# A hand-ordered fp32 encoder block: the fourth gate half's steps moved and spread, its two column blocks swapped, attention heads closer together, and the first projection's gated products kept in SBUF

## The chip, the cores and the metric

The kernel runs on one core of a Trainium2 chip. The metric is device time in microseconds (us); three runs of the kernel before gave 894.41, 894.84 and 895.23, median 894.84. One more run was recorded with a profile: it took 893.12, of which the profile's span is 891.3. All times below that are read off the trace count from the start of that span.

## The reference

One layer of a hybrid bidirectional encoder, for 256 tokens of width 2048, all in float32. A recurrent branch and an attention branch are projected, gated and summed, and the sum goes through an output projection.

```
z = rms_norm(x, norm_pre_w) @ w_in            # 2048 x 13312, split into the parts below
u_lru, g_lru, q, k, v, g_attn, m_lru, m_attn = split(z)
h   = rg_lru(conv(u_lru), forward) + rg_lru(conv(u_lru), backward)
y_a = h * silu(g_lru)                                   # branch A
y_b = windowed_gqa(rope(q), rope(k), v, sink) * silu(g_attn)   # branch B: 16 heads of 128, |i-j| <= 128
merged = sigmoid(m_lru) * (y_a @ w_proj_a) + sigmoid(m_attn) * (y_b @ w_proj_b)
out = x + rms_norm(merged @ w_out, norm_post_w)
```

## The kernel before, in words

**Precision.** Every float32 matrix is split into a high part that TensorE takes exactly (`wh`, a rounded copy made by ScalarE, line 219) and a low part (`wl`, the rest, made by VectorE, line 221). A product is three matmuls: high by high, high by low, low by high (`mm3`, lines 225 to 227). Weights are read once from HBM, so the kernel is a long stream of weight loads, splits and matmuls.

**Steps.** The order is written by hand in three lists, START, MERGE and OUT. An entry such as `p2.1` is one step: 1 MB of weights (128 x 2048 float32), used in two halves. The letters of MERGE: `p0` to `p3` are the four 512-column chunks of the first projection (`w_proj_a`), four steps each; `b0` to `b3` the same for the second (`w_proj_b`); `Am...` the fourth gate half, that is the upper 1024 columns of `m_attn`; `Om...` the first steps of the output projection. A `p` or `b` step is a "quad": 24 matmuls, and it counts as two ticks. An `Am` step is a "part": 12 matmuls and one tick. Steps are numbered through all three lists: `p0.0` is step 114, `b0.0` step 134, `b1.0` step 142, and the weight load of step 142 is called `raw142`, its split halves `wh142_0`, `wl142_0`, `wh142_1`, `wl142_1`.

**The gate halves.** The four halves L, M, N and A of the gate projections, and half of the output projection, multiply 2 x 2 blocks with seven products instead of eight (class `Seven`, m1 to m7). Sums of weight blocks that this needs are made by the DMA engines: a cell `x` is loaded by SyncE's queue (SP) and then the next block is added onto it in place by an accumulating DMA on GpSimd's queue (POOL, line 192: `Ax0a`, `Ax0b`, `Ax1a`, `Ax1b`, and the same for `y`). Sums of activation blocks lie in DRAM and come back through SP (line 337, `Am50`, `Am30`, ...). The seven products end in two column blocks of 512: the left one is complete with m2 (first tokens) and m4 (last tokens), the right one with m3 and m6, and m7.

**Around the steps.** `at(tick, fn)` puts other work at a tick: it is written into each engine's stream ahead of that tick's matmuls. Each engine runs its stream in order. For each step the load is issued three steps ahead (line 207, a ring of three 1 MB buffers `raw`), the cast four halves ahead, the subtraction three halves ahead. All other large tiles come from one pool of 45 slots, `units` (each 128 x 1024 float32); whoever gets a slot waits for the last reader of the tile that had it. What doesn't fit is parked in DRAM and fetched back (`park`, line 790, and `back`, line 794, both on SP).

**The merge.** `add_pa` (lines 940 to 946) multiplies a chunk of the first projection by its gate in the tile `tm[c]` and parks the result (`parkpa`); at `b{c}.0` it is fetched back as `pa` (line 1018). `add_pb` multiplies a chunk of the second projection by the gate `sm[c]` and adds `tm[c]` (VectorE, lines 951 and 952); one tick later `turn` transposes the sum on TensorE (line 963, tile `mt`). The heads of group c start at `p0.0` - 16 + 12c ticks, three ticks apart: `scores`, `expo` (VectorE, line 871), `exps` (ScalarE, lines 877 and 878), `normalise` (ScalarE, line 885), then `flip` on TensorE (line 891, tile `pt`), five ticks after the scores.

Of the kernel before, what the change touches and what calls it, by code (L numbers as in the profile page):

```python
# [21 lines left out]
P = 128  # L22
D = 2048
S = 256
# [6 lines left out]
DECAY = 12  # L31
SPIN = 10
HEAD0 = -16
STRIDE = 3
FIRST = 8
QAWAY = 10
QPARK = (0,)
# [1 line left out]
U0, GL0, Q0, K0, V0, GA0, ML0, MA0 = 0, 2048, 4096, 6144, 6656, 7168, 9216, 11264  # L39
# [14 lines left out]

MERGE = """p0.0 p0.1 p0.2 p0.3 p1.0 p1.1 p1.2 p1.3 p2.0 p2.1 p2.2 p2.3 Am1.0 p3.0 p3.1 Am1.1 p3.2 Am2.0 p3.3 Am2.1 b0.0
    Am5.0 b0.1 Am5.1 b0.2 Am3.0 b0.3 Am3.1 b1.0 b1.1 Am6.0 b1.2 Am6.1 b1.3 Am7.0 b2.0 Am7.1 b2.1 Am4.0 b2.2 Am4.1
    b2.3 b3.0 Om1.0 b3.1 Om5.0 b3.2 b3.3""".split()
OUT = """o2.0 o2.1 Om1.1 o2.2 Om5.1 Om2.0 o2.3 Om3.0 Om6.0 Om3.1 o3.0 Om6.1 Om2.1 o3.1 Om7.0 Om7.1 Om4.0 Om4.1  # L60
    o3.2 o3.3""".split()

# [8 lines left out]
QUADS = {"u": ("w_in", U0), "v": ("w_in", V0), "p": ("w_proj_a", 0),  # L71
         "b": ("w_proj_b", 0), "o": ("w_out", 0)}
PAIRS = {"g": GL0, "h": GA0, "w": U0, "k": K0, "q": Q0}
SEVENS = {"L": ("w_in", ML0 + 1024), "M": ("w_in", ML0), "N": ("w_in", MA0), "A": ("w_in", MA0 + 1024), "O": ("w_out", 0)}


PV_NORM = 0
# [9 lines left out]
def load_plan():  # L87

    plan = []
    for o in START + MERGE + OUT:  # L90
        a, i = o.split(".")
        if a[0] in SEVENS:
            plan.append(("part", a[0], a[1:], int(i)))
# [9 lines left out]
def content(p):  # L103
    if p[0] == "part":
        _, g, a, q = p
        m, c = SEVENS[g]
        b, f = SEVEN[a][2]
        return "part", m, c + f * 512, b, q
    return p


# [4 lines left out]
def body(ctx, tc, x, xT, wall, wlru, pvec, npost, ident_d, mask_d, rope_d, out):  # L116
# [18 lines left out]
    def half_unit(name, tag, dt=F32, bufs=2):  # L135
        return small.tile([P, 2, S], dt, tag=tag, name=name, bufs=bufs)
# [25 lines left out]
    def at(hs, fn):  # L162
        assert hs >= now[0], (hs, now[0])
        due.setdefault(hs, []).append(fn)

    first, last = {}, {}
# [7 lines left out]
    def soon(fn, d=1):  # L174
        at(now[0] + d, fn)
# [276 lines left out]
    xs = []  # L452
# [167 lines left out]
    sgl, sga = [], []  # L620
    ya, yb = [None] * 8, [None] * 8
# [117 lines left out]
    tm, sm, ms, msum = {}, {}, {}, {}  # L739


    def gate_unit(gates, c):
        if c not in gates:
            gates[c] = unit(f"mg{c}", F32, (P, 2, 512))
        return gates[c]

    def gated_out(gates, c, t):
        if t == 1 and (gates is tm or c < 2):
            soon(lambda: park("tm" if gates is tm else "sm", gates, c), 5)
# [7 lines left out]
    def combine(to, ps, other, sign):  # L757
        nc.vector.scalar_tensor_tensor(to, ps, float(sign), other, ALU.mult, ALU.add if sign > 0 else ALU.subtract)

    def gate_sum(gates, first=2):  # L760

        def done(t, c, ps, other, sign):
            to = gate_unit(gates, first + c)[:, t]

            def gate(src):
                nc.scalar.activation(to, src, AF.Sigmoid, scale=rtok[:, t:t + 1])
                gated_out(gates, first + c, t)

            if other is None:
                gate(ps)  # L770
            else:
                combine(to, ps, other, sign)
                soon(lambda: gate(to))
        return done
# [1 line left out]
    Seven("L", xs, None, gate_sum(tm))  # L776
    Seven("M", xs, None, gate_sum(tm, 0))
    Seven("N", xs, None, gate_sum(sm, 0))
    Seven("A", xs, None, gate_sum(sm))
    for n in range(8):  # L780
        behind(XSUM[n], lambda n=n: x_sums(n))

# [2 lines left out]
    def park(key, store, c):  # L785

        d = parked[key, c] = dram.tile([P, 1024], F32, name=f"park{key}{c}")
        t = store[c]
        store[c] = None
        nc.sync.dma_start(d, flat(t))  # L790

    def back(key, store, c, shape=(P, 2, 512)):
        store[c] = unit(f"{key}{c}", F32, shape)
        nc.sync.dma_start(flat(store[c]), parked[key, c])
# [58 lines left out]
    def head(hd, qh, ql, b, both, end):  # L853

        g, j = hd // 4, hd % 4
        sk = pv[:, PV_SINK + hd:PV_SINK + hd + 1]
        ts = [slice(t * P, (t + 1) * P) for t in range(2)]
        v = {}

        def scores():  # L860
            v["sc"] = bank(f"sc{hd}")
            for t in range(2):
                mm3(v["sc"][:, t], qh[:, j, ts[t]], ql[:, j, ts[t]], kv["kh"][:, g], kv["kl"][:, g], True, True)

        def expo():
            p = v["p"] = half_unit(f"p{hd}", "p")
            sc = v.pop("sc")
            m, nm, es = tiny(f"m{hd}"), tiny(f"nm{hd}"), tiny(f"es{hd}")
            dn = v["dn"] = tiny(f"dn{hd}")
            for t in range(2):  # L870
                nc.vector.tensor_tensor_reduce(p[:, t], sc[:, t], table["mask"][:, t], rtok_sc[:, t:t + 1], sk, ALU.add, ALU.max, m[:, t:t + 1])  # L871
            nc.vector.tensor_scalar(nm, m, -1.0, None, ALU.mult)  # L872
            soon(lambda: exps(p, nm, es, dn))

        def exps(p, nm, es, dn):
            for t in range(2):
                nc.scalar.activation(p[:, t], p[:, t], AF.Exp, bias=nm[:, t:t + 1], accum_out=dn[:, t:t + 1])  # L877
            nc.scalar.activation(es, nm, AF.Exp, bias=sk)
            v["es"] = es

        def normalise():
            dn, rd = v["dn"], tiny(f"rd{hd}")
            nc.vector.tensor_tensor(dn, dn, v["es"], ALU.add)
            nc.vector.reciprocal(rd, dn)
            soon(lambda: [nc.scalar.activation(v["p"][:, t], v["p"][:, t], AF.Copy, scale=rd[:, t:t + 1]) for t in range(2)])

        def flip():
            v["pt"] = bank(f"pt{hd}")
            for kt in range(2):
                for t in range(2):  # L890
                    nc.tensor.transpose(v["pt"][:, kt, ts[t]], v["p"][:, t, ts[kt]], ident)  # L891

        def p_parts():
            if j % 2 == 0:
                both.update({s: unit(f"p{s}{hd}", F32R, (P, 2, 2, S)) for s in "hl"})
            parts_of(both["h"][:, :, j % 2], both["l"][:, :, j % 2], v.pop("pt"))
            v.clear()

        def values():
            both["o"] = bank(f"o{hd}")  # L900
            ks = slice(g * P, (g + 1) * P)
            for kt in range(2):
                mm3(both["o"], kv["vh"][:, kt, ks], kv["vl"][:, kt, ks], both["h"][:, kt], both["l"][:, kt], kt == 0, kt == 1)

        def gate_out():
            y = sga[g][:, j - 1:j + 1]
            nc.vector.tensor_tensor(y, both["o"], y, ALU.mult)
            both.clear()
            if j == 3 and g < 2:
                soon(lambda: park("yb", sga, g), 4)  # L910

        for d, fn in ((0, scores), (1, expo), (3, normalise), (5, flip), (6, p_parts)):
            at(b + d, fn)
        if j % 2 == 1:
            at(b + 10, values)
            at(b + 11, gate_out)
            if g > 1:
                at(max(b + 12, end + hd // 2 - 6), lambda: yb_parts(hd // 2))

    def yb_parts(q):  # L920
        yb[q] = pair_unit(f"yb{q}")
        n = q % 2 * 2
        parts_of(yb[q][:, :, 0], yb[q][:, :, 1], sga[q // 2][:, n:n + 2])

    def heads(g, b, end):
        def start():
            h, l = unit(f"qh{g}", F32R), unit(f"ql{g}", F32R)
            parts_of(h, l, qs.pop(g))
            soon(lambda: back("sga", sga, g, (P, 4, S)), 6)
            for j in range(4):  # L930
                if j % 2 == 0:
                    both = {}
                head(4 * g + j, h, l, b + STRIDE * j, both, end)

        if g in QPARK:
            at(b - 8, lambda: back("q", qs, g, (P, 4, S)))
        at(b - 2, start)


    def add_pa(c):  # L940
        def done(t, ps):
            nc.vector.tensor_tensor(tm[c][:, t], ps, tm[c][:, t], ALU.mult)
            if t == 1:
                soon(lambda: park("pa", tm, c), 4)

        add_rows(f"pa{c}_", ya, done)

# [67 lines left out]
    at(tick["q0.0"] - 6, load_tables)  # L1015
    for c in range(4):
        at(tick[f"p{c}.0"], lambda c=c: back("tm", tm, c))
        at(tick[f"b{c}.0"], lambda c=c: back("pa", tm, c))
        if c < 2:
            at(tick[f"b{c}.0"], lambda c=c: back("sm", sm, c))  # L1020
        heads(c, tick["p0.0"] + HEAD0 + 4 * STRIDE * c, tick["b0.0"])
    for c in range(4):
        if c < 3:
            at(tick["p0.0"] - 8 + 2 * c, lambda c=c: back("ya", sgl, c, (P, 4, S)))
        if c < 2:
            at(tick["b0.0"] - 12 + 3 * c, lambda c=c: back("yb", sga, c, (P, 4, S)))
    for n in range(8):
        if n < 6:
            at(tick["p0.0"] - 3 + n, lambda n=n: y_parts(n))
        if n < 4:  # L1030
            at(tick["b0.0"] - 6 + n, lambda n=n: yb_parts(n))


    npt, xr, yw = [], [[], []], [[], []]
# [16 lines left out]
    b, n = ticks(), ticks(len(plan))  # L1051
# [64 lines left out]
    tick = -1  # L1116
# [94 lines left out]
```

## Time and profile before

| what | value |
|---|---|
| median of three runs | 894.84 us |
| the profiled execution, its own time | 893.12 us |
| its span | 891.3 us |
| TensorE busy in the span | 875.4 us (98%) |
| TensorE weight loads | 750.4 us (84%) |
| VectorE | 711.4 us (80%) |
| ScalarE | 643.2 us (72%) |
| moved by DMA | 247.94 MB, mean 278 GB/s |
| granted TensorE clock, mean | 0.993 |

To read it: TensorE is called PE in the rows, VectorE DVE, ScalarE ACT, SyncE SP; an engine with a q behind its name is its queue or sequencer. A row of the timeline has the start, the length, the engine, the source line, the operation, what it writes and reads, and in brackets how long the engine had been idle before it and what ended that. A DMA row of SP or POOL shows the issue alone, not the transfer.

### The profile page before, as it was taken

To read this page: it belongs to the slowest core of one execution; us is meant where nothing else is said; L and a number is where in the kernel's file an instruction comes from. 1 tells how busy PE (TensorE), PEld (TensorE's weight loads), DVE (VectorE), ACT (ScalarE), POOL (GpSimd) and SP (SyncE) were. 2 spreads that over 40 slices of the span, in tenths; PEclk is the share of its full clock that TensorE was granted. 3 is DMA by queue.
4 is the path that set the end of the run, shared out by engine and by line. 5 is a ranking of instruction groups with operands and counts; after the bars stand their busy time and mean duration, and the time that the engine had idled before them with its cause. 6 is when DMAs were issued, how large, how long until landed. Compare 5 with 4: busy or idle time off the path is not lost.

```text
span 891.3 us, 12379 instructions
## 1 busy us (share of the span) xinstructions
PE 875.4 (98%) x4542; PEld 750.4 (84%) x4542; DVE 711.4 (80%) x959; ACT 643.2 (72%) x937; POOL 72.5 (8%) x104
## 2 busy tenths in 40 slices
PE   9999999999999999999999999999999799999996
PEld 8888888888888888888888888888888588888885
DVE  6899999898897987799688778766767377787776
ACT  7689697968787886977875899955575265555754
POOL 0000000011001011100011100000101110000200
PEclk9999999999999999999999999999999989999998
DMA  9657699999869999969899965776989999999962
GB/s 345 254 189 259 208 366 233 361 335 290 285 226 297 308 297 318 322 241 277 282 350 308 301 241 206 256 280 235 297 269 294 296 306 293 293 330 368 236 179 95
DMA packets 55838, 247.94 MB, mean 278 GB/s; under 512 B 5856, under 2 KB 10720, under 8 KB 40288
## 3 DMA queue, kind: packets, MB, share of 16 engines
q1 hardware_dynamic: 43680, 204.42, 61.9%
q0 software_dynamic: 11520, 41.95, 24.3%
q8 instruction: 36, 0.59, 0.3%
q10 hardware_dynamic: 576, 0.76, 0.2%
q14 instruction: 26, 0.21, 0.1%
HBM read 230.33 MB, written 16.78 MB: 277 GB/s over the span
## 4 chain that ended last, share of the span: by engine, by line
PE 90%; DMA 5%; issue 4%; DVE 1%; POOLq 0%; ACT 0%; ACTq 0%; POOL 0%; DVEq 0%
PE ga L252 7%; PE gl L252 7%; PE q L252 7%; PE u L252 5%; DMA raw<-wall_dram 4%; PE ga L250 3%; PE gl L250 3%; PE q L250 3%; PE u L250 3%; PE k L252 2%; PE Nm L225 1%; PE Nm L226 1%; PE Lm L225 1%; PE Mm L225 1%; PE Mm L226 1%
## 5 line engine op out<-in xcount | busy, mean ns | idle before, releaser
L221 DVE TENSOR_TENSOR wl<-raw,wh 128x1024 fp32r<-128x1024 f32 (+1 forms) x252 | 299.3, 1203 | 73.0 <-ACT wh L219 62.6
L219 ACT CAST wh<-raw 128x1024 fp32r<-128x1024 f32 (+1 forms) x251 | 253.8, 1036 | 56.3 <-DMA raw<-wall_dram 49.1
L252 PE MATMUL ga<-xs,wh 128*128 128x512 f32 x256 | 63.5, 391 | 0.0
L252 PE MATMUL gl<-xs,wh 128*128 128x512 f32 x256 | 63.4, 391 | 0.0
L252 PE MATMUL q<-xs,wh 128*128 128x512 f32 x256 | 63.3, 391 | 0.0
L252 PEld LDWEIGHTS gl<-xs,wh 128*128 128x128 f32 x256 | 47.0, 188 | 9.0
L252 PEld LDWEIGHTS q<-xs,wh 128*128 128x128 f32 x256 | 46.9, 188 | 9.1
L252 PEld LDWEIGHTS ga<-xs,wh 128*128 128x128 f32 x256 | 46.7, 188 | 8.8
L252 PE MATMUL u<-xs,wh 128*128 128x512 f32 x192 | 47.5, 391 | 0.0
L252 PEld LDWEIGHTS u<-xs,wh 128*128 128x128 f32 x192 | 35.2, 188 | 6.7
L250 PE MATMUL q<-xs,wl 128*128 128x256 f32 x256 | 34.4, 283 | 0.0
L250 PEld LDWEIGHTS q<-xs,wl 128*128 128x128 f32 x256 | 33.2, 191 | 1.3
L250 PEld LDWEIGHTS ga<-xs,wl 128*128 128x128 f32 x256 | 33.0, 191 | 1.2
L250 PEld LDWEIGHTS gl<-xs,wl 128*128 128x128 f32 x256 | 32.8, 191 | 1.2
L250 PE MATMUL ga<-xs,wl 128*128 128x256 f32 x256 | 33.5, 283 | 0.0
L250 PE MATMUL gl<-xs,wl 128*128 128x256 f32 x256 | 33.2, 283 | 0.0
L871 DVE CUSTOM_DVE_ANT_0 p<-sc,table,pv 128x256 f32<-128x256 f32 x32 | 16.1, 542 | 13.9 <-PE sc L227 13.8
L250 PEld LDWEIGHTS u<-xs,wl 128*128 128x128 f32 x192 | 24.6, 191 | 0.9
L250 PE MATMUL u<-xs,wl 128*128 128x256 f32 x192 | 24.9, 283 | 0.0
L647 DVE SCALAR_TENSOR_TENSOR uu<-upad,pv,uu 128x256 f32<-128x256 f32 x48 | 23.2, 483 | 1.7
L148 ACT CAST ph<-pt 128x512 fp32r<-128x512 f32 x16 | 9.3, 583 | 20.3 <-PE pt L891 20.3
L877 ACT ACTIVATE p<-p,nm 128x256 f32<-128x256 f32 x32 | 16.0, 502 | 8.5 <-DVE nm L872 8.5
(545 smaller groups left out, 2308.6 us busy)
## 6 DMA issues: line engine op xcount, KB each, us to landing
raw<-wall_dram SPq DMA_DIRECT2D x121, 1024.0 KB, 7.5
lraw<-wlru_dram SPq DMA_DIRECT2D x8, 512.0 KB, 6.2
away<-xx SPq DMA_DIRECT2D x8, 512.0 KB, 8.2
Lm<-away SPq DMA_DIRECT2D x8, 512.0 KB, 13.3
Mm<-away SPq DMA_DIRECT2D x8, 512.0 KB, 13.9
Nm<-away SPq DMA_DIRECT2D x8, 512.0 KB, 14.0
Am<-away SPq DMA_DIRECT2D x8, 512.0 KB, 9.2
raw<-wall_dram SPq DMA_DIRECT2D x8, 256.0 KB, 5.2
```

What stands on the lines that cost most here:

```text
L148: nc.scalar.copy(h, src)
L219: cast(hs, raw)
L221: nc.vector.tensor_tensor(ls, raw, hs.bitcast(F32), ALU.subtract)
L225: nc.tensor.matmul(ps, wh, xh, start=start, stop=False, skip_group_check=more)
L226: nc.tensor.matmul(ps, wh, xl, start=False, stop=False, skip_group_check=more)
L250: nc.tensor.matmul(ps[:, 1], wl[:, sl], a[:, 0], start=False, stop=False)
L252: nc.tensor.matmul(ps, wh[:, sl], a, start=k == 0, stop=k == KT - 1)
L647: nc.vector.scalar_tensor_tensor(u, up[:, j, tap:tap + S], cw[:, tap:tap + 1], u, ALU.mult, ALU.add)
L871: nc.vector.tensor_tensor_reduce(p[:, t], sc[:, t], table["mask"][:, t], rtok_sc[:, t:t + 1], sk, ALU.add, ALU.max, m[:, t:t + 1])
L877: nc.scalar.activation(p[:, t], p[:, t], AF.Exp, bias=nm[:, t:t + 1], accum_out=dn[:, t:t + 1])
```

## The change

Five edits, all in the order of things; no matrix product is added or removed.

- `MERGE`: the first Am step stands after `p2.0` and not after `p2.3`, and the fourteen Am steps are spread to the last, `Am4.1`, behind `b3.0` and not behind `b2.2`. As before, `Om1.0` and `Om5.0` stand among the `b3` steps.
- The two column blocks of the fourth gate half are swapped: what the seven products complete with m2 and m4 is now chunk 3 of the gate and not chunk 2.
- The heads of a group stand at 0, 3, 5 and 8 ticks and the next group 11 ticks on, where it was 0, 3, 6, 9 and 12. The tiles of their probabilities come from two tags in turn.
- `tm[c]` with the first projection's gated products stays in its slot of `units`: four stores and four loads of 512 KB fall away.
- Loads of parked attention outputs (`yb`) and the splits of these outputs are put two or three ticks later.

```diff
-STRIDE = 3
+HEADS_AT = (0, 3, 5, 8, 11)
...
-MERGE = """p0.0 p0.1 p0.2 p0.3 p1.0 p1.1 p1.2 p1.3 p2.0 p2.1 p2.2 p2.3 Am1.0 p3.0 p3.1 Am1.1 p3.2 Am2.0 p3.3 Am2.1 b0.0
...
+MERGE = """p0.0 p0.1 p0.2 p0.3 p1.0 p1.1 p1.2 p1.3 p2.0 Am1.0 p2.1 p2.2 Am1.1 p2.3 Am2.0 p3.0 p3.1 Am2.1 p3.2 Am5.0 p3.3
...
-SEVENS = {"L": ("w_in", ML0 + 1024), "M": ("w_in", ML0), "N": ("w_in", MA0), "A": ("w_in", MA0 + 1024), "O": ("w_out", 0)}
+SEVENS = {"L": ("w_in", ML0 + 1024), "M": ("w_in", ML0), "N": ("w_in", MA0), "A": ("w_in", MA0 + 1536), "O": ("w_out", 0)}
...
-        return "part", m, c + f * 512, b, q
+        return "part", m, c + (-512 if g == "A" else 512) * f, b, q
...
-    def gate_sum(gates, first=2):
+    def gate_sum(gates, first=2, step=1):
...
-            to = gate_unit(gates, first + c)[:, t]
+            to = gate_unit(gates, first + step * c)[:, t]
...
-    Seven("A", xs, None, gate_sum(sm))
+    Seven("A", xs, None, gate_sum(sm, 3, -1))
...
-            p = v["p"] = half_unit(f"p{hd}", "p")
+            p = v["p"] = half_unit(f"p{hd}", ("p", "uu")[hd % 2])
...
-                at(max(b + 12, end + hd // 2 - 6), lambda: yb_parts(hd // 2))
+                at(max(b + 12, end + hd // 2 - 4), lambda: yb_parts(hd // 2))
...
-                head(4 * g + j, h, l, b + STRIDE * j, both, end)
+                head(4 * g + j, h, l, b + HEADS_AT[j], both, end)
...
             nc.vector.tensor_tensor(tm[c][:, t], ps, tm[c][:, t], ALU.mult)
-            if t == 1:
-                soon(lambda: park("pa", tm, c), 4)
...
-        at(tick[f"b{c}.0"], lambda c=c: back("pa", tm, c))
...
-        heads(c, tick["p0.0"] + HEAD0 + 4 * STRIDE * c, tick["b0.0"])
+        heads(c, tick["p0.0"] + HEAD0 + HEADS_AT[4] * c, tick["b0.0"])
...
-            at(tick["b0.0"] - 12 + 3 * c, lambda c=c: back("yb", sga, c, (P, 4, S)))
+            at(tick["b0.0"] - 9 + 2 * c, lambda c=c: back("yb", sga, c, (P, 4, S)))
...
-            at(tick["b0.0"] - 6 + n, lambda n=n: yb_parts(n))
+            at(tick["b0.0"] - 4 + n, lambda n=n: yb_parts(n))
```

**SP's queue ahead of `raw142`**, the weights of `b1.0`. Before, from the load that `b0.2` uses (`raw138`) on; `Ay...` are plain first loads of the cells `y`, `Am30` and `Am31` activation sums:

```order
L207 DMA raw138_6666<-wall_dram 128x2048
L194 DMA Ay0a_6668<-wall_dram 128x1024
L194 DMA Ay0b_6669<-wall_dram 128x1024
L337 DMA Am30_6672<-away0_74 128x1024
L790 DMA parkpa3_6702<-tm3_6285 128x1024
L207 DMA raw140_6737<-wall_dram 128x2048
L194 DMA Ay1a_6739<-wall_dram 128x1024
L194 DMA Ay1b_6740<-wall_dram 128x1024
L337 DMA Am31_6743<-away1_75 128x1024
L207 DMA raw142_6801<-wall_dram 128x2048
```

The same stretch of SP's queue in the change, where `b0.2` is step 139 and `b1.0` still step 142:

```order
L194 DMA Ay0a_6594<-wall_dram 128x1024
L194 DMA Ay0b_6595<-wall_dram 128x1024
L337 DMA Am30_6598<-away0_74 128x1024
L794 DMA sm0_6646<-parksm0_5695 128x1024
L207 DMA raw139_6689<-wall_dram 128x2048
L207 DMA raw140_6714<-wall_dram 128x2048
L194 DMA Ay1a_6716<-wall_dram 128x1024
L194 DMA Ay1b_6717<-wall_dram 128x1024
L337 DMA Am31_6720<-away1_75 128x1024
L207 DMA raw142_6781<-wall_dram 128x2048
```

`parkpa3` is gone, the fetch of the gate `sm0` has come in, and the two loads `Ay0a` and `Ay0b` stand ahead of two weight loads instead of behind one.

**ScalarE around the seventh head** (`p6`, in group 1). Before, from the exponentials of `p5` to the scaling of `p6` that its transposes wait for; `ya`, `ph` and `qh` are high parts of the branch output, of the transposed probabilities and of q:

```order
L219 COPY wh116_1_5546<-raw116_5455 128x1024
L148 COPY ya5_5564<-ya2_5346 128x2x256
L148 COPY ph4_5566<-pt4_5535 128x2x256
L219 COPY wh117_0_5583<-raw117_5492 128x1024
L885 ACTIVATE p5_5500<-p5_5500,rd5_5569 128x256 x2
L219 COPY wh117_1_5619<-raw117_5492 128x1024
...
L219 COPY wh118_0_5650<-raw118_5562 128x1024
L148 COPY ph4_5566<-pt5_5638 128x2x256
L219 COPY wh118_1_5679<-raw118_5562 128x1024
L148 COPY qh2_5697<-q2f_4895 128x1024
L885 ACTIVATE p6_5606<-p6_5606,rd6_5667 128x256 x2
```

In the change, the end of the same stretch:

```order
L219 COPY wh117_1_5638<-raw117_5505 128x1024
L148 COPY qh2_5656<-q2f_4895 128x1024
L148 COPY ph4_5550<-pt5_5621 128x2x256
L841 COPY q3f_5263<-q3r_5333 32x256 x4
L885 ACTIVATE p6_5556<-p6_5556,rd6_5626 128x256 x2
L219 COPY wh118_0_5674<-raw118_5583 128x1024
```

The scaling of `p6` has moved ahead of the two casts of step 118, and nothing else that stood behind it has come in ahead of it.

**TensorE at the transposes of the same head.** Before and in the change, the rows on both sides of them (a matmul of the first projection reads a half of its step's weights, named by `wh`):

```order
L227 MATMUL pa0__5520<-wh117_0_5583,ya6_4101 128x512
L891 MATMUL pt6_5727<-ident_95,p6_5606 128x128 x4
L225 MATMUL pa0__5520<-wh117_1_5619,ya7_4744 128x512
```

```order
L227 MATMUL pa0__5535<-wh116_0_5531,ya4_5548 128x512
L891 MATMUL pt6_5690<-ident_95,p6_5556 128x128 x4
L225 MATMUL pa0__5535<-wh116_1_5567,ya5_5585 128x512
```

The transposes have moved two half steps up, past 24 matmuls of 128 x 512.

More of the change, by code (lines that the diff above doesn't have):

```diff
@@ L53 @@
 }
-MERGE = """p0.0 p0.1 p0.2 p0.3 p1.0 p1.1 p1.2 p1.3 p2.0 p2.1 p2.2 p2.3 Am1.0 p3.0 p3.1 Am1.1 p3.2 Am2.0 p3.3 Am2.1 b0.0
-    Am5.0 b0.1 Am5.1 b0.2 Am3.0 b0.3 Am3.1 b1.0 b1.1 Am6.0 b1.2 Am6.1 b1.3 Am7.0 b2.0 Am7.1 b2.1 Am4.0 b2.2 Am4.1
-    b2.3 b3.0 Om1.0 b3.1 Om5.0 b3.2 b3.3""".split()
+MERGE = """p0.0 p0.1 p0.2 p0.3 p1.0 p1.1 p1.2 p1.3 p2.0 Am1.0 p2.1 p2.2 Am1.1 p2.3 Am2.0 p3.0 p3.1 Am2.1 p3.2 Am5.0 p3.3
+    b0.0 Am5.1 b0.1 Am3.0 b0.2 b0.3 Am3.1 b1.0 Am6.0 b1.1 b1.2 Am6.1 b1.3 Am7.0 b2.0 b2.1 Am7.1 b2.2 Am4.0 b2.3 b3.0
+    Am4.1 Om1.0 b3.1 Om5.0 b3.2 b3.3""".split()
 OUT = """o2.0 o2.1 Om1.1 o2.2 Om5.1 Om2.0 o2.3 Om3.0 Om6.0 Om3.1 o3.0 Om6.1 Om2.1 o3.1 Om7.0 Om7.1 Om4.0 Om4.1
@@ L758, in combine @@
         nc.vector.scalar_tensor_tensor(to, ps, float(sign), other, ALU.mult, ALU.add if sign > 0 else ALU.subtract)
-    def gate_sum(gates, first=2):
+    def gate_sum(gates, first=2, step=1):
         def done(t, c, ps, other, sign):
-            to = gate_unit(gates, first + c)[:, t]
+            to = gate_unit(gates, first + step * c)[:, t]
             def gate(src):
                 nc.scalar.activation(to, src, AF.Sigmoid, scale=rtok[:, t:t + 1])
-                gated_out(gates, first + c, t)
+                gated_out(gates, first + step * c, t)
             if other is None:
```

## The prediction

> **What bounds the kernel now.** I read the page first, then the busy time by stretches of 20 us, the timeline of TensorE where a stretch is not full, and the chain that ended last through that place.
>
> ```profile
> span 891.3 us, 12379 instructions
> PE 875.4 (98%) x4542; PEld 750.4 (84%) x4542; DVE 711.4 (80%) x959; ACT 643.2 (72%) x937; POOL 72.5 (8%) x104
> ```
>
> TensorE is busy for 98% of the span, and the change takes no matmul away and adds none. So it can win only idle time of TensorE, or time at a lower clock. All but two of the 20 us stretches have TensorE busy for their full 20.00 us at a granted clock of 1.00: the one at the end of the span, which the change doesn't reach, and the second of these:
>
> ```profile
> 680.00:700.00 20.00, 20.00 (x90) 16.57 (x89) 10.26 (x10) 7.47 (x9) 4.27 (x5) 1.00 1.05 286
> 700.00:720.00 20.00, 12.84 (x46) 9.71 (x45) 11.37 (x15) 7.11 (x9) 0.86 (x1) 0.83 1.03 348
> ```
>
> The columns are TensorE, its weight loads, VectorE, ScalarE and GpSimd, then the granted clock, the DMA share and GB/s. From 700 to 720 TensorE is idle for 7.16 us and the clock is down to 0.83, with the DMA engines full (1.03) before and during it. The timeline of TensorE shows three waits in it:
>
> ```profile
> 702.38 0.39 PE L226 MATMUL pb__6635<-wl,yb 128*128 128x512 f32 x1
> 702.61 0.39 PE L227 MATMUL pb__6635<-wh,yb 128*128 128x512 f32 x1
> 703.66 0.47 PE L225 MATMUL Am<-wh,Am 128*128 128x512 f32 x1 [0.67 <-DMA Am<-away]
> ...
> 706.26 0.39 PE L227 MATMUL Am<-wh,Am 128*128 128x512 f32 x1
> 712.28 0.47 PE L963 MATMUL mt<-ident,sm 128*128 128x128 f32 x1 [5.64 <-DVE sm L952]
> 713.61 0.90 PE L963 MATMUL mt<-ident,sm 128*128 128x128 f32 x3 [0.86 <-DVE sm L952]
> ```
>
> The transposes `mt` wait for `sm` on VectorE. The chain says why VectorE is late with it:
>
> ```profile
> 681.98 26.52 DMA raw<-wall_dram
> ...
> 708.60 1.05 ACT wh L219
> ...
> 709.68 1.23 DVE wl L221
> 710.90 0.61 DVE sm L951
> ...
> 714.52 0.43 PE pb__6909 L225
> ...
> 718.78 0.28 PE pb__6909 L226
> ```
>
> A weight load (`raw142`, for `b1.0`) takes 26.52 us to land. VectorE runs in order, and the subtraction `wl` that needs these weights stands ahead of `sm`, whose data was long there. So the bound in this stage is the DMA engines, and it reaches TensorE through the order of VectorE.
>
> **What this place costs.** Ends of matmuls are modelled, so I take starts; at full clock neighbours stand 0.23 us apart (702.38 and 702.61). 703.66 - 702.61 - 0.23 = 0.8; 712.28 - 706.26 - 0.23 = 5.8; 713.61 - 712.28 less one transpose of some 0.1 = 1.2. Together **7.8**. Then ten matmuls from 714.52 to 718.78 at 0.43 in place of 0.23 lose 2.0, and three transposes in 0.90 lose half of it, 0.4: **2.4**. If the place vanished whole, it would give 10.2 us.
>
> The page "TensorE: Matmul & The Clock Gate" of the Trainium skill (section "What's actually happening") says that an idle window of some 3.4 us halves the clock until as long a busy one has passed. The trace agrees for one gap: 0.43 against 0.23 us behind 5.8 us of waiting, and behind the 0.8 us eleven matmuls in the 2.6 us from 703.66 to 706.26, still at 0.24. By that rule a new wait under 3.4 us would cost itself alone, a longer one 2 us more; the sum below doesn't use it.
>
> **The DMA queue, which the change moves.**
>
> ```profile
> q1 hardware_dynamic: 43680, 204.42, 61.9%
> q0 software_dynamic: 11520, 41.95, 24.3%
> ```
>
> The columns are packets, MB and share of the span, for SP's queue and for the accumulating one of POOL. 0.619 x 891.3 / 204.42 = 2.70 us of all engines per MB, so 1.42 for a 512 KB transfer and 2.83 for a 1 MB load; 0.243 x 891.3 / 41.95 = 5.16 per MB, so 2.71 for a 512 KB accumulation, nearly twice as much.
>
> ```profile
> 665.58 0.33 SPq L794 DMA_DIRECT2D pa<-parkpa  x1
> ...
> 673.63 0.42 SPq L790 DMA_DIRECT2D parkpa<-tm  x1
> 674.10 0.42 SPq L207 DMA_DIRECT2D raw<-wall_dram  x1
> ```
>
> ```profile
> 672.99 0.89 POOL L192 DMA_DIRECT2D Ax0a<-wall_dram  x1 [28.09 <-DVE wl L221]
> ...
> 698.43 0.86 POOL L192 DMA_DIRECT2D Ay1a<-wall_dram  x1 [5.45 <-DVE wl L221]
> ```
>
> Does this price explain the late load? From 674 to its landing at 708.5 the engines had, by the order of SP given above, `Ay0b`, `Am30`, `parkpa3`, `Ay1a`, `Ay1b`, `Am31` (6 x 1.42), `raw140` and `raw142` (2 x 2.83), and seven accumulations from 672.99 to 698.43 (19.0): 33.2 us of work in 34.5. It does, with a factor of 1.04.
>
> **The change, part by part.**
>
> *Products kept on chip.* Eight transfers go, 8 x 1.42 = 11.3 us of DMA work, but only `parkpa3` lies in the 34.5 us, and `pa0` just ahead of it. Alone they would bring `raw142` in 1.5 to 3 us sooner. The four slots that the products keep are a rival, below.
>
> *The fourth gate half sooner.* Of the seven accumulations, `Ax0a` and `Ax0b` now belong to a step that comes some 15 us sooner and are over by 666. In the new order `Ay0a`, first of the ten rows shown, waits for a slot that `p3.2` still reads, until about 666. From there to `raw142` SP has `Ay0a`, `Ay0b`, `Am30`, `sm0`, `Ay1a`, `Ay1b`, `Am31` (7 x 1.42), `raw139`, `raw140` and `raw142` (3 x 2.83), and POOL four accumulations and perhaps half of a fifth: 9.9 + 8.5 + 10.8 to 12.2 = 29.3 to 30.6, by 1.04 makes 30 to 32 us: `raw142` lands at 696 to 698. Until when is there time? Now 3.7 us pass from its landing (708.5) to the first `mt` (712.28), and TensorE would be at `mt` at 706.26 + 0.23 - 0.8 = 705.7: so until 702. That leaves 4 to 6 us, and I take the whole wait as gone, with its clock. `Am31`, the 0.8, is in the queue ahead of `raw142` and lands sooner too. What is late next is `sm` itself, whose data comes half a tick ahead: I put 0.2 for this, between the 0.86 of the second wait above and the nothing of the group that comes next, four transposes in 0.60 with no wait noted:
>
> ```profile
> 721.87 0.60 PE L963 MATMUL mt<-ident,sm 128*128 128x128 f32 x4
> ```
>
> *Heads closer.* ScalarE is what they lean on.
>
> ```profile
> 500.00:570.00 70.00, 70.00 (x389) 60.89 (x388) 57.00 (x107) 67.18 (x119) 0.87 (x1) 1.00 0.70 240
> ```
>
> ```profile
> 562.52 0.91 ACT L885 ACTIVATE p<-p,rd 128x256 f32<-128x256 f32 x2
> ...
> 570.69 0.90 ACT L885 ACTIVATE p<-p,rd 128x256 f32<-128x256 f32 x2
> ```
>
> ```profile
> 565.76 0.60 PE L891 MATMUL pt<-ident,p 128*128 128x128 f32 x4
> 575.15 0.60 PE L891 MATMUL pt<-ident,p 128*128 128x128 f32 x4
> ```
>
> With 67.18 of 70 us busy it is full from 500 to 570, so there a shift counts in full. These rows are the sixth and seventh heads: scaled by 563.4 and 571.6, transposed at 565.8 and 575.2, leads of 2.3 and 3.6 us. In the change the seventh's transposes come 24 matmuls sooner, 24 x 0.23 = 5.5 us, at 569.7; its scaling has only two casts fewer ahead of it, 2 x 1.05 = 2.1 (`wh` in the chain above), and ends at 569.5. The lead shrinks from 3.6 to 0.2 us: no wait, but nothing left. Bounds: 0, and 2.3 if the sixth head's lead, that of the tightest chain now, were used up again; I take 0. The later heads stand where ScalarE (the fourth column) has room:
>
> ```profile
> 600.00:700.00 100.00, 100.00 (x470) 83.25 (x469) 69.41 (x106) 59.28 (x98) 9.56 (x11) 1.00 0.88 275
> ```
>
> *Columns swapped, `yb` later.* Chunk 3 of the gate is now complete with `Am4.1`, behind `b3.0`, and is read behind `b3.3`; the splits of `yb` stand four ticks, some 11 us, ahead of `b0.0`. Matmuls between hide both: 0.
>
> **Sum.** 893.12, the profiled run's own time (its span of 891.3 and 1.8 around it), less 10.2, plus 0.2, is 883.1. The median of the runs is 894.84, 1.7 above that run, so I add 1.7: **884.8**. Its own range is 883.2 to 888, with the 2.3 of the heads inside.
>
> **Rivals.**
>
> *The shortage comes back later (888 to 892.9).* The last accumulations of the gate half, `Ax1a` and `Ax1b` for `Am4`, now stand behind `Ox0a` and `Ox0b` in POOL's order and meet the loads for `Om1.0` and `b3.1`. From 731 on SP has nine such items, 4 x 1.42 + 5 x 2.83 = 19.8, POOL five to six, 13.6 to 16.3: 33 to 36, by 1.04 up to 37.5, so `raw158` lands at 766 to 769. It is needed at about 774. Were the DMA engines 1.3 times as slow as their rows, it would land at 778: 4 us of wait and 2.4 of clock, 891. For it speaks that ScalarE already waits for a load here; against it, that TensorE follows 6 us behind.
>
> ```profile
> 778.08 1.05 ACT L219 CAST wh<-raw 128x1024 fp32r<-128x1024 f32 x1 [2.80 <-DMA raw<-wall_dram]
> ```
>
> *The change doesn't do what it says (893 to 896.6).* The bytes of the gate half are the same, so if `raw142` is served only behind all seven accumulations still, the two transfers of 1.42 are all that is won: 2 to 3 us less wait, 892 to 893, and a small wait at the seventh head takes it back. The section "Queues, rings and completion order" of "DMA: Bandwidth & Descriptors" in the Trainium skill says that each DMA engine goes round its queues packet by packet; by that, a load beside accumulations always shares, and spreading them only spreads the slow loads, which would give this case. That 33.2 us of work filled 34.5 fits it, and so the order of issue has to bring the relief, as worked out above.
>
> *Slots (slower, about 901).* The products keep four of 45 slots from `p1` to `b3`. From `b1.1` to `b2.3` a low part of the weights waits for a slot whose last reader stands only 23 to 26 matmuls, 5.2 to 5.9 us, ahead of the matmul that needs it; the tightest before is 27. If VectorE had more than 4 us of other work in that time (the 1.2 of the subtraction is needed too), each chunk would stall: three chunks, by 3 us and 2.4 of clock each, 16 us, 901. Against it: VectorE has a quarter of this stage free.
>
> ```profile
> 714.00:780.00 66.00, 66.00 (x289) 54.23 (x288) 48.59 (x59) 37.58 (x47) 6.95 (x8) 0.96 0.96 295
> ```
>
> **How the numbers follow.** Forecast 0.66, shortage later 0.14, no relief 0.08, slots or something else on that side 0.12. A measurement of this kernel can tell about 0.2%, 1.8 us, from no change. Faster by more than that: 0.66 + 0.14 = 0.80; within it 0.08; slower 0.12. The range runs from 883.2 to 892.5: nearly all of the first two cases, and the rest stays out.
>
> **What would show it.** Right: TensorE full from 700 to 720, a clock of 1.00 there, `raw142` landing in under 20 us, no wait for `sm` above 0.3 us. Wrong: a wait at `pt` near 569, a wait of ScalarE for a load that reaches TensorE near 775, or gaps from 715 to 760 that a subtraction `wl` ends.

## The result, and the profile after

The change takes 883.89 us (median of four runs, 883.02 to 884.32) where the kernel before took 894.83: a ratio of 0.9877 (95% interval 0.986 to 0.9894), 10.9 us less. The forecast was 884.8. The recorded execution took 884.32 with a span of 882.5 us; from this step's sum it should have been 883.1.

The lines of the page that answer to those of before, and the stretch that was short of work, with the one near 350 that will matter below (columns as before):

```profile
span 882.5 us, 12373 instructions
...
PE 872.6 (99%) x4542; PEld 748.5 (85%) x4542; DVE 712.8 (81%) x959; ACT 644.4 (73%) x937; POOL 72.5 (8%) x104
```

```profile
340.00:360.00 20.00, 19.18 (x111) 16.66 (x111) 13.53 (x15) 12.03 (x21) 3.48 (x4) 1.00 1.05 321
700.00:720.00 20.00, 19.99 (x93) 16.34 (x92) 15.09 (x21) 10.68 (x15) 1.76 (x2) 1.00 1.04 317
```

From 700 to 720 TensorE is busy for 19.99 of 20 us at full clock, where it had 12.84 at 0.83. The DMA engines are as full there as they were (1.04). What has changed is when they do their work: ahead of this stretch they had time to spare before (a share of 0.82 from 660 to 680), and have none in the change (1.01). Before, then the change:

```profile
660.00:680.00 20.00, 20.00 (x92) 16.55 (x91) 16.82 (x21) 14.64 (x20) 1.83 (x3) 1.00 0.82 272
```

```profile
660.00:680.00 20.00, 20.00 (x90) 16.57 (x89) 13.73 (x17) 14.62 (x19) 2.55 (x4) 1.00 1.01 329
```

On SP's queue, ScalarE, VectorE and TensorE, these are the four links of the chain that was the bound:

```profile
683.47 0.42 SPq L207 DMA_DIRECT2D raw<-wall_dram  x1
```

```profile
698.81 2.00 ACT L219 CAST wh<-raw 128x1024 fp32r<-128x1024 f32 x2 [4.50 <-DMA raw<-wall_dram]
```

```profile
699.89 1.23 DVE L221 TENSOR_TENSOR wl<-raw,wh 128x1024 fp32r<-128x1024 f32 x1 [2.63 <-ACT wh L219]
704.37 0.69 DVE L949 TENSOR_TENSOR sm<-pb__6657,sm 128x512 f32<-128x512 f32 x1 [3.25 <-PE pb__6657 L227]
...
706.42 0.69 DVE L950 TENSOR_TENSOR sm<-tm,sm 128x512 f32<-128x512 f32 x1
707.03 1.22 DVE L221 TENSOR_TENSOR wl<-raw,wh 128x1024 fp32r<-128x1024 f32 x1
```

```profile
706.66 0.39 PE L227 MATMUL Am<-wh,Am 128*128 128x512 f32 x1
706.89 0.82 PE L961 MATMUL mt<-ident,sm 128*128 128x128 f32 x4
```

`raw142` is issued at 683.47 and cast from 698.81: 15.3 us in place of 26.5. The subtraction `wl` is over 3.25 us before the data of `sm` is there, and the first transpose `mt` follows the last `Am` matmul after 0.23 us, with no wait.

### The profile page after: what moved, and what is told of

Its sections match the earlier page's. It is cut to its first block, busy times and chain, and to the rows that moved or that the text cites. A ratio compares the mean times of both kernels' runs of the same rounds, so it can differ in the third digit from the quotient of the medians.

```text
span 882.5 us, 12373 instructions
## 1 busy us (share of the span) xinstructions
PE 872.6 (99%) x4542; PEld 748.5 (85%) x4542; DVE 712.8 (81%) x959; ACT 644.4 (73%) x937; POOL 72.5 (8%) x104
## 4 chain that ended last, share of the span: by engine, by line
PE 84%; DMA 5%; issue 4%; DVE 3%; ACT 3%; POOLq 0%; ACTq 0%; DVEq 0%; POOL 0%
PE q L252 7%; PE ga L252 5%; PE gl L252 5%; DMA raw<-wall_dram 4%; PE u L252 4%; PE q L250 3%; PE ga L250 3%; PE gl L250 2%; PE u L250 2%; DVE wl L221 2%; PE k L252 2%; PE Am L225 1%; PE Am L227 1%; PE Nm L227 1%; PE Nm L225 1%
## 5 line engine op out<-in xcount | busy, mean ns | idle before, releaser
L250 PEld LDWEIGHTS q<-xs,wl 128*128 128x128 f32 x256 | 33.2, 191 | 1.3
L250 PE MATMUL gl<-xs,wl 128*128 128x256 f32 x256 | 33.2, 283 | 0.0
L871 DVE CUSTOM_DVE_ANT_0 p<-sc,table,pv 128x256 f32<-128x256 f32 x32 | 16.1, 541 | 10.4 <-PE sc L227 10.3
L731 ACT ACTIVATE sig<-sg 128x512 f32<-128x512 f32 x16 | 10.2, 637 | 14.2 <-DVE sg L574 14.2
```

Of the source, the lines that this page charges most:

```text
L250: nc.tensor.matmul(ps[:, 1], wl[:, sl], a[:, 0], start=False, stop=False)
L731: nc.scalar.activation(sg, dst, AF.Sigmoid)
```

## The experiments

Two quantities serve for all of them. The **lead** is the time from the cast of `raw142` to the point at which TensorE would reach `mt` (start of the last `Am` matmul, plus 0.23): before, 706.49 - 708.60 = -2.1 us; in the change, 706.89 - 698.81 = 8.1. The **loss** is what TensorE lost in this stage: its steps from start to start, less the median step of that kind of matmul in the kernel before, summed from `b0` to `b1`: 10.4 us before, 0.25 in the change (no run has less). A ratio is always to the kernel before on the same chip.

**The new order alone.** The kernel before with the diff of MERGE and of the column blocks, and nothing else.

> The kernel before with only the new order of MERGE and the swapped column blocks; products are still parked and fetched, heads stay three ticks apart, yb stays early. Theory (the order of issue relieves the DMA queue): from the landing of Ay0a's slot on, SP and POOL have what they have in the change plus pa0 and parkpa3, 2 x 1.42 us; raw142 landed at 698.8 in the change, so here at 701 to 702, still ahead of the 703 from which TensorE would wait. Stall gone, 883 to 886 us. Rival (the products kept on chip do it): 892 to 895, with a wait for sm of 4 us or more near 706.

Measured: 886.14 us, 0.9905 (0.989 to 0.992). The load is cast 4.6 us ahead of TensorE's arrival, the loss is 0.4:

```profile
703.55 1.05 ACT L219 CAST wh<-raw 128x1024 fp32r<-128x1024 f32 x1 [4.14 <-DMA raw<-wall_dram]
```

```profile
708.15 0.96 PE L963 MATMUL mt<-ident,sm 128*128 128x128 f32 x4
```

The order by itself takes the stall away: it brings `raw142` 6.7 us sooner against TensorE, and the DMA engines are full from 660 to 680 here too (0.96). The load is cast at 703.55, where I had expected it at 701 to 702, and the time is just above my range of 883 to 886. A second wait, of 1.1 us, has appeared elsewhere; it comes back with the heads below.

**The products alone.**

```diff
-            if t == 1:
-                soon(lambda: park("pa", tm, c), 4)
...
-        at(tick[f"b{c}.0"], lambda c=c: back("pa", tm, c))
```

> The kernel before with only the products of the first projection kept on chip, so that eight transfers of 512 KB fall away. Theory: one to two of them lay ahead of raw142, so it lands 1.5 to 3 us sooner, at 705.5 to 707, and the wait for sm shrinks from 5.6 us by as much: 891 to 893 us. Rival (these transfers were the cause): raw142 lands before 702 and the time is 884 to 886. Second rival (the four slots cost more than the transfers): slower than 895.

Measured: 893.05 us, 0.9984 (0.997 to 0.9997); lead -1.5, loss 9.1. The time lies at the upper edge of the expected range (0.05 us above it), but the reason was missed: against TensorE the load came 0.6 us sooner and not 1.5 to 3. SP's queue of this kernel, what it waited for, and its DMA engines show why; in the window rows the last three columns are the granted clock, the DMA share and GB/s:

```profile
663.95 0.33 SPq L337 DMA_DIRECT2D Am<-away  x1
669.88 0.33 SPq L794 DMA_DIRECT2D sm<-parksm  x1
670.31 1.39 SPq L207 DMA_DIRECT2D raw<-wall_dram  x1
```

```profile
SPq L794 <- PE pa__6295 L227: 5.8, 1, 5.8
```

```profile
666.00:671.00 5.00, 5.00 (x25) 4.13 (x24) 2.09 (x4) 3.11 (x4) 0.00 (x0) 1.00 0.21 69
```

In the kernel before, whose TensorE is 1 us ahead here, the same fetch of `sm0` went out at 666.01, and the DMA share was 0.71:

```profile
665.00:670.00 5.00, 5.00 (x26) 4.12 (x25) 2.09 (x4) 3.74 (x5) 0.00 (x0) 1.00 0.71 252
```

With the products in their slots, `sm0` gets one some 3 us later against TensorE: its fetch waits 5.8 us, for a matmul at the end of the first projection, and the weight load behind it on SP's queue waits too. The engines are nearly idle just ahead of the stretch in which they are short, and most of what the dropped transfers save is lost.

**Products and heads closer, and all but the order.** First the diff of the heads on top of the one above; then those two and the later `yb`.

> The kernel before with the products kept on chip and the heads closer together, nothing else. With the products alone raw142 landed 1.5 us behind TensorE's arrival at mt, with heads and yb as well 2.5 us ahead of it. In the run with the products alone the fetch of sm0 was issued 3 us later than before, which fits a wait for a slot that held SP's queue. Theory (heads that end sooner give slots back sooner, so SP's queue isn't held): nearly all of that 4 us comes from the heads: 889 to 891. Rival (the later yb loads and splits did it): 892 to 894, with a wait of 4 us or more at mt.

> The change without its new order: products kept, heads closer, yb later, but the steps of MERGE and the column blocks as before. Theory: as with the products alone, 890 to 893, since heads and yb are hidden by matmuls. Rival (the parts work together, or the heads win time of their own): below 888. If the closer heads cost something that the order hides, 893 to 896 with waits at pt near 569.

Products and heads: 893.69 us, 0.9991 (0.9976 to 1.0007), lead -1.4, loss 8.6. My theory fell, and the rival came true: closer heads do not give the slot back sooner (DMA share from 666 to 672: 0.39). With `yb` later as well: 889.7 us, 0.9943 (0.9926 to 0.996), lead 2.4, loss 2.6; the share of the same stretch (669 to 675, since TensorE is 3.7 us later in that run) is 0.63, and `sm0` goes out 2.6 us sooner against TensorE. That time is better than my theory's 890 to 893 and short of the rival's 888. So it was the later loads and splits of `yb`, at least on top of the other two; by themselves they were not run. That they do it by giving slots back in another order fits the earlier `sm0`, but is not shown further. The waits of 1.12 and 1.00 in place of 5.64 and 0.86 leave the clock at full:

```profile
712.14 0.33 PE L961 MATMUL mt<-ident,sm 128*128 128x128 f32 x1 [1.12 <-DVE sm L950]
713.47 0.55 PE L961 MATMUL mt<-ident,sm 128*128 128x128 f32 x3 [1.00 <-DVE sm L950]
```

**The change with the products parked again.**

> The change with the products parked and fetched again, all else as in the change. Theory: raw142 lands 2.8 us later than in the change, at 701 to 702, ahead of 703: no stall, 883 to 886 us. Rival (the slots or transfers decide): a wait for sm near 705 or later waits of TensorE, 888 or more.

Measured: 887.03 us, 0.9919 (0.9903 to 0.9936); lead 3.1, loss 1.9. My theory of no stall fell, by little: the load is cast at 704.73 and not at 701 to 702, and there are waits of 0.40 and 1.00 at `mt`. On top of everything else the products are worth 5 us of lead, not the 2.8 that I had put down, but only 1.6 us of loss, because the rest of the lead is slack. This run also stands below the order alone (lead 4.6): without the kept products, closer heads and later `yb` together cost 1.5 us of lead where on the old order, with the products kept, they gave 3.9.

**The change with heads three ticks apart.**

> The change with the heads three ticks apart again, from one tag. Theory (slots): raw142 lands 2 to 4 us later against TensorE than in the change, but still ahead of the 3.8 us that are needed: no stall at mt, 883.5 to 886, perhaps 1.3 us at 643 as in the run with the new order alone. Rival (the closer heads carry a part of the gain with the new order too): 887 or more.

Measured: 886.57 us, 0.9909 (0.9888 to 0.9931), between the theory and the rival; lead 7.5, loss 0.25. There is nothing at `mt`, as the theory said, but there are two new waits, 0.5 at 620 and this one, which the run with the order alone had as well:

```profile
643.72 0.39 PE L227 MATMUL Am<-wh,xs 128*128 128x512 f32 x1
645.22 0.50 PE L225 MATMUL o<-ph,vh 128*128 128x512 f32 x1 [1.12 <-DVE m L871]
```

```profile
640.68 1.29 DVE L942 TENSOR_TENSOR tm<-pa__6023,tm 128x512 f32<-128x512 f32 x2 [1.86 <-PE pa__6023 L227]
641.89 2.35 DVE L221 TENSOR_TENSOR wl<-raw,wh 128x1024 fp32r<-128x1024 f32 x2
644.16 0.54 DVE L871 CUSTOM_DVE_ANT_0 p<-sc,table,pv 128x256 f32<-128x256 f32 x1
```

With the old spacing and the new order, the `values` of one pair of heads (tile `o`) wait for VectorE to be through with the next head's scores, and VectorE is busy with `tm` and two `wl`. The closer heads step out of this. From 600 to 650 TensorE loses 2.4 us without them and 0.1 with them. (The run also takes back the second tag of the probabilities; the two were not tried apart.)

**VectorE's order alone.** In the kernel before, `wl142_0` is written behind the operations on `sm`:

```diff
+                if hs == 282:
+                    split(284, only="l")
-                if hs > FIRST:
+                if hs > FIRST and hs != 281:
                     split(hs + 3, only="l")
```

> The kernel before with one edit on VectorE: the subtraction wl of the first half of step 142 stands behind the four operations on sm and not ahead of them. The landing of raw142 stays where it is. Theory (the DMA queue is the bound, VectorE's order only passes it on and adds to it): the transposes mt run at once, near 706.3, and TensorE then waits for wh and wl of the same load, to about 710.9, some 4 us in all in place of 7.0: 891 to 892.5 us. If both waits are short enough to leave the clock at 1.00, up to 2.4 us less: 889. Rival (the order on VectorE is the cause): no wait is left, 884 to 886.

Measured: 889.61 us, 0.9946 (0.9924 to 0.9967); the load is as late as before (lead -2.1), and the loss is 3.9:

```profile
707.22 0.82 PE L963 MATMUL mt<-ident,sm 128*128 128x128 f32 x4
710.41 0.49 PE L225 MATMUL pb__6909<-wh,yb 128*128 128x512 f32 x1 [2.38 <-ACT wh L219]
711.67 0.50 PE L226 MATMUL pb__6909<-wl,yb 128*128 128x512 f32 x1 [0.77 <-DVE wl L221]
712.01 0.40 PE L227 MATMUL pb__6909<-wh,yb 128*128 128x512 f32 x1
712.25 0.39 PE L225 MATMUL pb__6909<-wh,yb 128*128 128x512 f32 x1
```

Both halves of the theory hold. The late load alone costs 3.6 us, which this order on VectorE does not take away; the old order adds 3.4 more of waiting, and 2.4 of slow clock, for here the next matmuls follow at 0.23 us. Waits of 2.4 and 0.8 us leave the clock as it is; behind the wait of 5.6 in the kernel before, matmuls stood 0.43 us apart for some 4 us. That is the window rule of "TensorE: Matmul & The Clock Gate" in the Trainium skill ("What's actually happening"), and the runs agree with it. No run has a wait between 2.4 and 5.0 us, so where the limit lies is not shown.

**Two accumulations left out.** In the kernel before, the two accumulations at 672.99 and 675.92 are left out; the fourth gate half is then computed without one block.

```diff
-                load(self.cell(m, q), p, True)
+                if (self.name, m, q) != ("A", "m6", 0):
+                    load(self.cell(m, q), p, True)
```

> The kernel before, with the two accumulations into the cell x that were issued at 673 and 676 (for the first Am6 step) left out, so that the fourth gate half is computed without one block; the order of everything else is unchanged. Theory (the accumulations ahead of raw142 are the larger part of the shortage, 2.71 us each by the queue's share): raw142 lands 5.4 us sooner, near 703, about 2.8 us ahead of TensorE's arrival at mt; a wait of 1 us at the first mt and 1.2 behind it is left, the clock stays, 885.5 to 887.5 us. Rival (an accumulation costs a load of raw142 no more than a plain transfer of its bytes): 2.8 us sooner, a wait of 3.5 to 4 us, 889 to 891.

Measured: 884.63 us, 0.9897 (0.988 to 0.9913); lead 6.3 and no wait, with every other instruction at its place in the order:

```profile
701.23 2.00 ACT L219 CAST wh<-raw 128x1024 fp32r<-128x1024 f32 x2 [5.45 <-DMA raw<-wall_dram]
```

```profile
707.30 0.39 PE L227 MATMUL Am<-wh,Am 128*128 128x512 f32 x1
707.54 0.82 PE L964 MATMUL mt<-ident,sm 128*128 128x128 f32 x4
```

Without these two accumulations the stall is gone: `raw142` comes 8.4 us sooner against TensorE, 4.2 for each and not the 2.71 of the queue's share. The time is 0.9 us better than the range of my theory, which had used 2.71.

**Extra stores.** In the change, two or six more stores of 512 KB on SP just ahead of `raw142`:

```diff
+        if lead == 3 and i == 142:
+            for n in range(6):
+                nc.sync.dma_start(dram.tile([P, 1024], F32, name=f"extra{n}"), flat(tm[0]))
```

> The change with six extra stores of 512 KB (a finished tile to DRAM, read by nobody) on SP's queue just ahead of raw142. Theory: TensorE reached mt 8.2 us behind the landing of raw142 in the change, and 3.8 of these are needed for cast, subtraction and sm; six stores at 1.42 us bring it 8.5 us later, so the slack of 4.4 is used up and a wait of about 4 us stands at mt, with slower matmuls behind it if the clock drops: 888 to 890.5 us. Rival (the landing isn't what binds, or stores pass beside loads for nothing): 883 to 885.

> The change with two extra stores of 512 KB ahead of raw142. The six stores brought its landing 12.5 us later, 2.1 each, more than the 1.42 that I had taken. Theory (a slack of some 4.4 us, then a wait that grows one for one): two stores take 2.8 to 4.2 us of the slack and cost nothing, 883.5 to 885.5. Rival (no slack, every store costs its share of the 11.6 us that six cost): 887 to 888.5.

Six: 895.54 us, 1.0011 (0.9999 to 1.0023), the whole gain gone and 5 us above my range; lead -4.9, loss 11.9. The wait is 8.4 us in place of the 4 expected. Its TensorE:

```profile
715.00 0.47 PE L964 MATMUL mt<-ident,sm 128*128 128x128 f32 x1 [8.39 <-DVE sm L953]
716.33 0.90 PE L964 MATMUL mt<-ident,sm 128*128 128x128 f32 x3 [0.85 <-DVE sm L953]
```

Two: 886.17 us, 0.9924 (0.9895 to 0.9953), lead 4.4, one wait of 0.34 and a loss of 0.6. The time is 2 us above the change's on the same chip, between the two theories, with intervals that overlap; the stage shows the first, a slack that two stores nearly use up. The recorded run lost another 3.7 us near 350, ahead of the edit, which is the place of the next experiment. Six stores used 13.0 us of lead, two 3.7: 1.9 to 2.2 each, and not 1.42.

Sorted by lead, the runs make one curve (us); the one with VectorE's order mended (lead -2.1, loss 3.9) stands off it, since there less hangs on the load:

| run | lead | loss at the stage |
|---|---|---|
| six stores | -4.9 | 11.9 |
| before | -2.1 | 10.4 |
| products; products and heads | -1.5; -1.4 | 9.1; 8.6 |
| all but the order | 2.4 | 2.6 |
| products parked again | 3.1 | 1.9 |
| two stores | 4.4 | 0.6 |
| order alone | 4.6 | 0.4 |
| two accumulations left out | 6.3 | 0.25 |
| tables earlier (the next experiment) | 6.7 | 0.25 |
| heads three ticks apart; the change, in both recorded runs | 7.5; 8.1 | 0.25 |

Above some 4.8 us a lead is worth nothing more (the change's 8.1 less the 3.25 that its VectorE stands idle ahead of `sm`); below, waiting grows as the lead falls, and in the runs with waits of 5.0 us and more the slow clock adds its 2.4.

**The wait near 350, and a faster version.** The recorded run of the change waits here, in code that the change does not touch:

```profile
351.24 0.39 PE L225 MATMUL gate<-ul,lwh 128*128 128x256 f32 x1 [0.82 <-ACT gi L671]
```

ScalarE computes `gi` behind a cast that has waited for a late load:

```profile
349.40 1.05 ACT L219 CAST wh<-raw 128x1024 fp32r<-128x1024 f32 x1 [7.06 <-DMA raw<-wall_dram]
```

The edit fetches the mask and rope tables earlier, out of this stretch:

```diff
-    at(tick["q0.0"] - 6, load_tables)
+    at(tick["q0.0"] - 30, load_tables)
```

> The change itself once more, beside the three kernels that follow, as their measure. 883 to 885 us by every theory; the wait near 350, which lies in code that the change doesn't touch, may be anything from 0.1 to 1.5 us.

> The change with one more edit: the mask and rope tables (two loads of 256 KB) are fetched 30 ticks ahead of q0.0 and not 6, so that they leave the stretch from 329 to 348, in which the DMA engines are full, for one in which they are busy for 0.6 to 0.7. Theory (the wait of 0.98 us near 350 is the same kind of shortage, a late load whose cast stands ahead of the work that TensorE waits for): that wait goes, 882 to 883.5 us, 1 us below the change. Rival (another transfer takes their place, or the slot that is held longer delays something): same as the change, or slower.

The change again: 884.11 us, 0.9895 (0.988 to 0.991), recorded at 883.17 with no wait near 350. Tables earlier: 884.45 us, 0.9903 (0.9886 to 0.9919), no wait there either. The time misses the theory's 882 to 883.5, and no faster version came of it. In the recorded runs TensorE lost between 0.1 us (before) and 4.6 us (all but the order) near 350, and 1.2 in the change. Whether the tables shift that range can't be told from one recorded run each.

## Why the prediction was right, and where it was not

**The place and its worth.** Right. The loss at the stage fell from 10.4 to 0.25 us, where the sum took off 10.2 and gave 0.2 back. The 0.2 is there too: the transposes take 0.82 us where the next group takes 0.60 (at 713.03), since the second of the four, at 707.17, follows VectorE's last operation on `sm`, which ends at 706.42 + 0.69 = 707.11. The 1.2 us by which the recorded run is above the sum are the wait near 350, 1.1 more than in the kernel before; the sum had taken all other stretches as full. (The first 20 us are not full either, with TensorE busy for 18.73; the prediction's "all but two" overlooks them, but the change doesn't reach them.) That the median, 883.89, is nevertheless 0.9 below the forecast is in part luck: the forecast added 1.7 because the recorded run of the kernel before lay below its median, and the change's lies 0.4 above its own. The kernel before had lost next to nothing near 350 in its recorded run, which may be why; it was recorded only once.

**Why the load was late.** Right: the accumulations, through VectorE's order. Leaving two out removes the stall, and mending VectorE's order alone leaves 3.9 us.

**When it lands.** Forecast 696 to 698, cast at 698.81. The start of the count was early: `Ay0a` went out at 667.64 and not at 666, and `Ax0b`, "over by 666", was issued at 664.44 and took 5.7 us. Slack was forecast at 4 to 6 us; it is 3.3, the idle time of VectorE ahead of `sm`.

```profile
667.64 0.33 SPq L194 DMA_DIRECT2D Ay0a<-wall_dram  x1
```

```profile
Ax0b<-wall_dram POOLq DMA_DIRECT2D x1, 512.0 KB, 5.7
```

**The price of a transfer.** Too low where it was used one by one. The sum over the stretch (33.2 us of work in 34.5) held, but a store cost 1.9 to 2.2 us of lead in place of 1.42 and an accumulation 4.2 in place of 2.71. The DMA views give the two queues (packets, MB, share of the stretch), in the kernel before from 675 to 708 and in the change from 675 to 700:

```profile
q0 software_dynamic: 989, 3.65, 55.6%
q1 hardware_dynamic: 1192, 5.70, 46.2%
```

```profile
q1 hardware_dynamic: 1110, 5.83, 59.4%
q0 software_dynamic: 599, 2.19, 44.2%
```

In the change a MB costs about what it did (0.594 x 25 / 5.83 = 2.55 us; 0.442 x 25 / 2.19 = 5.05). But SP's queue has only a part of the engines while the accumulations run beside it: 46% before, 59% in the change. This is the sharing that "Queues, rings and completion order" in "DMA: Bandwidth & Descriptors" of the Trainium skill describes; that it is done packet by packet no run here shows. For a store in the change the share gives 1.42 / 0.594 = 2.4, a little above the 1.9 to 2.2 measured. For an accumulation in the kernel before it gives 2.71 / 0.462 = 5.9, well above the measured 4.2. So a transfer costs more than its own work, but how much more these shares do not settle. The rival built on the sharing ("no relief") fell: `Ax0a` and `Ax0b`, the second landed at 670.1 in the change, could share nothing with a load that was issued at 683.47.

**Products kept: "1.5 to 3 us sooner" alone.** Wrong. Alone it was 0.6, because a fetch that waits for a slot held SP's queue; on top of the other edits it was 5. The step that failed looked for the cost of the four slots at the low parts of the weights, and not on the queue where the weight loads stand behind such a fetch.

**Heads closer: 0.** Right for the change, wrong as a value of the edit. The seventh head's lead was to shrink to 0.2; its scaling and transposes stand at

```profile
570.31 0.91 ACT L885 ACTIVATE p<-p,rd 128x256 f32<-128x256 f32 x2
```

```profile
571.24 0.60 PE L891 MATMUL pt<-ident,p 128*128 128x128 f32 x4
```

which is 0.02 us, without a wait. That so little was enough is luck as well. But the step asked only what closer heads could cost. With the new order and the old spacing TensorE loses 2.4 us from 600 to 650, and the edit is what avoids that.

**Columns swapped, `yb` later: 0.** No run takes one of these out of the change, so that they are worth 0 there is not shown; with 3.3 us of slack it is likely for a small shift. On the old order the later `yb` is what brought the lead from -1.4 to 2.4, so as a value of the edit 0 was wrong.

**The rivals.** The shortage did not come back later. The loads for `Om1.0` and `b3.1` are cast here, the second within the last row without a wait:

```profile
763.31 1.05 ACT L219 CAST wh<-raw 128x1024 fp32r<-128x1024 f32 x1 [2.19 <-DMA raw<-wall_dram]
770.57 2.96 ACT L219 CAST wh<-raw 128x1024 fp32r<-128x1024 f32 x3
```

From 700 to 780 TensorE is busy for 79.98 of 80 us, so no slot stalls it from `b1.1` to `b2.3` either.

## What to carry to other kernels

Turn a stall behind a transfer into a lead (arrival of the reader less landing) and ask how much lead is needed. In time, parts looked nearly worthless (the products alone, 1.2 us) or nearly sufficient (the order alone, 8.1 of 10.9 us), because waiting stops once the lead is enough. The leads of parts need not add up either: the products gave 0.6 us of lead alone and 5.0 on top of the rest. So take a part out of the whole change as well as putting it in alone. A transfer on queues that share the DMA engines cost more here than its own work, 1.9 to 2.2 us for 1.42 and 4.2 for 2.71; and on an in-order queue a fetch that waits for a buffer holds back the loads behind it. When a mended order on the reading engine is cheap, try it: here three lines on VectorE gave 5 us, of the 10.9 of the change, without touching a transfer.

## What was not expected

The same unchanged stretch near 350 lost 0.1 to 4.6 us in different recorded runs, more than half of what some of the edits are worth; one recorded execution is not enough to take a stretch in which the DMA engines are full (1.05 here) as one without waits. And a kernel can stand on its edge without a loss: the seventh head's transposes start 0.02 us after the data that they read.
